# RWKV and mLSTM in one trunk kernel: the layout of the inverse blocks, the rows of the low rate weights, and the place of a normalisation

## The chip, the cores and the metric

The kernel runs on one core of one Trainium2 chip. The metric is the device time of one execution, from its start to its end, in microseconds (us). An execution that was recorded with the hardware profiler also has a span, from its first to its last instruction.

## The reference, cut to what matters

The program computes one decoder layer for a prompt (16 meta tokens and 1024 rows) and for eight sample sequences of eight rows, with model width 1024. One input projection feeds two mixers. Their gated sum goes through an output projection, a layer norm, a convolutional feed-forward block and a second layer norm. Everything is float32. Three pieces of it bear on this change.

```python
def _head_norm(h, eps):                      # mLSTM: over the 256 values of a head and row
    mu = jnp.mean(hf, -1, keepdims=True)
    var = jnp.mean(jnp.square(hf - mu), -1, keepdims=True)
    return (hf - mu) * lax.rsqrt(var + eps)
...
h = num / jnp.maximum(jnp.abs(den), jnp.exp(-m_row))[..., None]      # mLSTM, then _head_norm
...
w_log = -jax.nn.softplus(-(w0 + jnp.tanh(xw) @ w2)) - 0.5            # RWKV rates: rank 64
a = jax.nn.sigmoid(a0 + xa @ a2)                                     # rank 64
...
S = S * w[:, :, None, :] + sa[..., None] * (kk * a)[:, :, None, :] + v[..., None] * k[:, :, None, :]
```

The RWKV recurrence on the last line runs over all rows for 16 heads of 64. The kernel does it in chunks of 64 rows, and for that it needs the inverse of a unit triangular 64x64 matrix for each head and chunk.

## The kernel before, in words

**Passes.** The 1090 rows that count (sample, meta, prompt) are worked in three passes of up to 384 columns. Weights are split into a high part of type fp32r and a low remainder, and a dense product is three matmuls (high by high, high by low, low by high), called by `mm3`, which ends in line 57. So nearly all matmuls have line 57 in the profile, and are told apart by their tiles.

**Stage one, 0 to about 420 us: mLSTM.** For each pass and each of four heads `mlstm_qkv` makes q, k and v (dense products into the PSUM tile `d`), and `mlstm_head` works three tiles of 128 rows. For a tile it forms the weighted scores `wt`, the sum of the inner and the carried part into `hraw` (line 552, VectorE), and the new state `C1` (line 577, VectorE, read by the next tile's matmul). When the three tiles are done, the head is normalised: mean and variance of each tile (lines 585, 586), the denominators of all three tiles at once in four small VectorE operations (590 to 593), one power of -1/2 on GpSimd (594), and a subtract and multiply for each tile (596). Then TensorE transposes the tiles (606, 612), ScalarE scales them, and they go to HBM. In this stage the framework's list scheduler orders the instructions of every engine by its own model of their times; the order of the program is the priority. In all, 12 heads and 36 tiles are worked.

**Stage two, about 420 to 1610 us: RWKV with the gates.** Two of the 8 blocks of 128 channels make one unit `u`, so there are 4 units in each of 3 passes, 12 in all. The order on TensorE is written out by hand here (`rwkv`): a loop over units, each of 18 rounds, in which one step of the recurrence (`rwkv_chain`), pieces of the preparation of later units (`rwkv_g`, `rwkv_t`, `rwkv_mid`) and a share of the dense products (`dense`) are issued one after the other. The other engines are ordered by the list scheduler.

- `rwkv_k` loads the rank-64 weights of a block into `raw`, which holds them twice, in rows 0 to 63 and again in rows 64 to 127. ScalarE rounds all 128 rows of 256 columns into the high part (line 690), and GpSimd makes the low part in two instructions of 64 rows by 128 columns (693).
- `rwkv_r` forms the two rate products of a block (decay and in-context rate). The input `xwa[n]` holds the high part of the inputs in one half of the rows and the low part in the other. Each product is a matmul over 128 rows with the high weights, and one over 64 rows with the low weights (the loop of lines 715 to 719). There are 24 blocks, so 48 matmuls of each of the two forms.
- `rwkv_t` inverts the 32x32 diagonal blocks on VectorE (`LX`, lines 838 to 850). `rwkv_mid` transposes them (890, 892), forms the off-diagonal blocks on TensorE into the PSUM tile `gg`, and collects the inverse in `TT`. For that ScalarE copies with lines 918, 919 and 921. The tile is laid out as (2, 32, 12): a column of one 64x64 inverse is 12 elements, 48 bytes, from the next.
- `rwkv_chain` runs 6 steps for a unit. A step multiplies the right-hand side `Rs` by the inverse: four matmuls of 64x64 with `TT` as the stationary operand, in the loop over `up`. The profile has two records for a float32 matmul, so that is 8 records, 72 times. The matmuls of `VU` by `Gk` have the same form, 64x64 with 64 moving columns, and their stationary operand lies contiguous in SBUF.

**Stage three, to the end:** output projection, layer norms and the feed-forward block. The change does not touch it.

Of the kernel before, what the change touches and what calls it, by code (L numbers as in the profile page):

```python
# [8 lines left out]
F32 = mybir.dt.float32  # L9
F32R = mybir.dt.float32r  # L10
AF = mybir.ActivationFunctionType
ALU = mybir.AluOpType
# [31 lines left out]
class Trunk:  # L44
# [468 lines left out]
    def mlstm_head(self, pas, h, pool):  # L513
# [14 lines left out]
        for t in range(NT):  # L528
            c0, n = self.tcols(pas, t)
            cs = slice(c0, c0 + n)  # L530
            first = pas == 0 and t == 0
            ps = self.gh()
            fb = self.psc.tile([P, 512], F32, name="u")
            self.mm(ps[0:n, 0:n], k[:, cs], q[:, cs])
            self.mm(fb[0:n, 0:n], sel[:, h, 0:n], self.frow[:, cs])
            wt = pool.tile([P, 128], F32, name="wt", bufs=3)
            mask = self.const("tri0", slice(0, 90)) if first else self.const("tri")
            nc.vector.scalar_tensor_tensor(wt[0:n, 0:n], fb[0:n, 0:n], CT[0:n, t, 0, h:h + 1], mask,
                                           op0=ALU.add, op1=ALU.add)
            nc.scalar.activation(wt[0:n, 0:n], wt[0:n, 0:n], AF.Exp)  # L540
            nc.vector.tensor_tensor(wt[0:n, 0:n], ps[0:n, 0:n], wt[0:n, 0:n], op=ALU.mult)
            pn = self.psc.tile([P, 512], F32, name="y", bufs=2)
            self.mm(pn[0:n, 0:257], wt[0:n, 0:n], V1[0:n, t, 0:257])
            pi = self.psc.tile([P, 512], F32, name="y", bufs=2)
            if first:
                for b in range(8):
                    self.mm(pi[0:n, 0:257], self.qm[:, b * 90:(b + 1) * 90], C0[:, b, 0:257], b == 0, b == 7)
            else:
                self.mm(pi[0:n, 0:257], q[:, cs], C1[:, h, 0:257])
            it = pool.tile([P, 258], F32, name="it", bufs=3)  # L550
            nc.scalar.activation(it[0:n, 0:257], pi[0:n, 0:257], AF.Copy, scale=CT[0:n, t, 1, h:h + 1])
            nc.vector.tensor_tensor(hraw[0:n, t, 0:257], pn[0:n, 0:257], it[0:n, 0:257], op=ALU.add)

            pk = self.gh()
            nc.tensor.transpose(pk[0:n, 0:128], k[:, cs], ident)
            if first:
                wm = pool.tile([P, 9], F32, name="wm")
                nc.vector.tensor_scalar(wm[0:n, :], self.const("rm9", slice(0, n)), CT[0:n, t, 3, h:h + 1], None, op0=ALU.mult)
                km = pool.tile([P, 9, 128], F32, name="km")
                nc.vector.tensor_tensor(km[0:n], pk[0:n, 0:128].unsqueeze(1).broadcast_to([n, 9, 128]),  # L560
                                        wm[0:n].unsqueeze(2).broadcast_to([n, 9, 128]), op=ALU.mult)
                for b in range(9):
                    pc = self.psc.tile([P, 512], F32, name="u") if b % 2 else self.pst.tile([P, 512], F32, name="t")
                    self.mm(pc[:, 0:257], km[0:n, b, :], V1[0:n, t, 0:257])
                    if b < 8:
                        nc.vector.scalar_tensor_tensor(C0[:, b, 0:257], C0[:, b, 0:257], dec[:, h, NM + b:NM + b + 1],
                                                       pc[:, 0:257], op0=ALU.mult, op1=ALU.add)
                    else:
                        nc.scalar.copy(C1[:, h, 0:257], pc[:, 0:257])
                nc.sync.dma_start(out=self.o["C_s"][h], in_=C0[:, :, 0:257])  # L570
            else:
                tm = t - 1 if pas == 0 else t
                kw = pool.tile([P, 128], F32, name="kw", bufs=2)
                nc.scalar.activation(kw, pk[:, 0:128], AF.Copy, scale=CT[:, t, 3, h:h + 1])
                pc = self.pst.tile([P, 512], F32, name="t")
                self.mm(pc[:, 0:257], kw, V1[:, t, 0:257])
                nc.vector.scalar_tensor_tensor(C1[:, h, 0:257], C1[:, h, 0:257], dec[:, h, tm:tm + 1],
                                               pc[:, 0:257], op0=ALU.mult, op1=ALU.add)
        if pas == NPASS - 1:
            nc.sync.dma_start(out=self.o["C_p"][h], in_=C1[:, h, 0:257])  # L580

        mv = pool.tile([P, 3, 2], F32, name="mv", bufs=2)
        for t in range(NT):
            st = pool.tile([P, 6], F32, name="bst", bufs=2)
            nc.vector.bn_stats(st, hraw[:, t, 0:256])
            nc.vector.bn_aggr(mv[:, t, :], st)
        dn = pool.tile([P, 3], F32, name="dn", bufs=2)
        den = hraw[:, 0:NT, 256]
        stt = nc.vector.scalar_tensor_tensor
        stt(dn[:, 0:NT], den, -1.0, den, op0=ALU.mult, op1=ALU.max)  # L590
        nc.vector.tensor_tensor(dn[:, 0:NT], dn[:, 0:NT], CT[:, 0:NT, 2, h], op=ALU.max)
        stt(dn[:, 0:NT], dn[:, 0:NT], LN_EPS, dn[:, 0:NT], op0=ALU.mult, op1=ALU.mult)
        nc.vector.tensor_tensor(dn[:, 0:NT], dn[:, 0:NT], mv[:, 0:NT, 1], op=ALU.add)
        nc.gpsimd.tensor_tensor(dn[:, 0:NT], dn[:, 0:NT], self.const("mhalf")[:, 0:NT], op=ALU.pow)
        for t in range(NT):
            nc.vector.tensor_scalar(hraw[:, t, 0:256], hraw[:, t, 0:256], mv[:, t, 0:1], dn[:, t:t + 1],
                                    op0=ALU.subtract, op1=ALU.mult)
        off = W * pas
        for cb in range(2):
            j = 2 * h + cb  # L600
# [55 lines left out]
    def rwkv_static(self, pool):  # L656
        nc = self.nc
        r = {}
        r["TT"] = [pool.tile([P, 2, 32, 12], F32, name=f"TT{n}") for n in range(2)]
        for t in r["TT"]:  # L660
            nc.gpsimd.memset(t, 0.0)
        r["Gd"] = pool.tile([P, 404], F32, name="Gd")
        nc.gpsimd.memset(r["Gd"], 0.0)
        r["LX"] = pool.tile([P, 32, 32], F32, name="LX")
        r["n2"] = pool.tile([P, 32], F32, name="n2")
        nc.vector.memset(r["n2"], 0.0)
        self.ones = pool.tile([P, 128], F32R, name="ones")
        nc.scalar.copy(self.ones, self.const("bones"))
        self.r = r
# [6 lines left out]
    def rwkv_k(self, pas, j, w, pool):  # L676

        nc, i = self.nc, self.i
        m = j % 2
        st = self.st[pas, j] = {}  # L680
        RA = pool.tile([P, NP, 4, 64], F32, name="RA", bufs=6)
        KB = pool.tile([P, NP, 4, 64], F32, name="KB", bufs=6)

        one, two = slice(0, 4, 3), slice(1, 3)
        rs, bs = (two, one) if m else (one, two)
        st.update(RA=RA, KB=KB, r=RA[:, :, rs, :], k=KB[:, :, rs, :], a=RA[:, :, bs, :], b=KB[:, :, bs, :])
        raw = self.wpool.tile([P, 512], F32, name="raw", bufs=3)[:, 0:256]
        nc.sync.dma_start(out=raw, in_=i["lora2"][j, :, 0:256])
        lw = [self.rs.tile([P, n], F32R, name=f"lw{n}", bufs=2) for n in (256, 128)]
        nc.scalar.copy(lw[0], raw)  # L690
        for q in (0, 64):
            a, c = slice(q, q + 64), slice(2 * q, 2 * q + 128)
            nc.gpsimd.tensor_tensor(lw[1][a], raw[a, c], lw[0][a, c].bitcast(F32), op=ALU.subtract)
        yield from self.lerp(pas, w, 8 + j, self.pt[:, j, 1:2], self.pd[:, j, 1:2], st["k"], pool)
        st["lw"] = lw

    def rwkv_r(self, pas, j, w, pool):
# [15 lines left out]

        zs = self.gbank()
        for n in range(2):
            rows = slice(64 * n, 64 * n + 64)
            x, ps = self.xwa[n], zs[:, n, 0:W]
            self.mm(ps, lw[0][:, 2 * rows.start:2 * rows.start + 128], x, True, False)
            self.mm(ps, lw[1][rows], x[rows], False, True)
        for n, (dst, bias) in enumerate(((cw, dv(3)), (ta, dv(4)))):  # L720
            act(dst, zs[:, n, 0:W], AF.Tanh, bias=bias, scale=0.5)
        for _ in range(4):
# [157 lines left out]
    def rwkv_mid(self, pas, u, pool):  # L880
# [34 lines left out]

        yield from (m0 + 0.11 for _ in product(A21, Tn, 0, 32, lambda w, h1: nc.scalar.copy(P1[h1], w[h1])))
        for q in (0, 64):
            nc.scalar.copy(TT[q:q + 32, 0, :, cs], Tx[q:q + 32, :, cs])
        nc.scalar.copy(TT[:, 1, :, cs], Tx[:, :, cs])
        yield m0 + 0.165  # L920
        yield from (m0 + 0.22 for _ in product(P1, Tx, 32, 0, lambda w, h0: nc.scalar.copy(
            TT[h0, 1, :, cs].rearrange("p t c -> p c t"), w[h0])))
        if pas == 0:

            yield m0 + 0.23
# [17 lines left out]
    def rwkv_chain(self, pas, u, pool):  # L943
# [30 lines left out]
        for p in range(NP):  # L974
            nxt = []
            for e in range(2):
# [30 lines left out]
                up, sp = yr[:, 256:384], yr[:, 384:512]  # L1007
                for h in range(2):
                    for m in range(2):
                        self.mm(up[brs[m], hh[h]], TT[brs[m], :, :, 6 * m + h * NP + p], Rs[brs[m], hh[h]], meta, True, True)  # L1010
                for m in range(2):
                    nc.scalar.copy(now[m][0][brs[m], e, :], up[brs[m], :])
                if p + 1 < NP:
# [715 lines left out]
```

## Time and profile before

| | |
|---|---|
| three timed runs | 2534.26 us median (2525.82 to 2535.51) |
| the profiled execution, its time | 2531.55 us |
| the profiled execution, its span | 2529.8 us, 43736 instructions |
| TensorE matmuls busy | 2361.2 us (93%), mean granted clock 0.968 of full speed |
| TensorE weight loads busy | 2125.8 us (84%), beside the matmuls |
| VectorE busy | 1549.8 us (61%) |
| ScalarE busy | 1078.4 us (43%) |
| GpSimd busy | 481.2 us (19%) |
| DMA | 356.97 MB, mean 141 GB/s |

In the rows of the profile PE is a TensorE matmul, PEld a weight load, DVE VectorE, ACT ScalarE and POOL GpSimd. A row of a timeline gives the start in us from the beginning of the span, the length in us, engine, line, operation, the tile written, the tiles read, the part of the TensorE array that is used, the shape and the number of records merged into the row. What stands in brackets is how long the engine sat idle before it, and what ended that. "issue" is idle time for which the profile shows no wait.

### The profile page before, as it was taken

The numbers are of one execution on the slowest core, as the hardware profiler recorded it, in microseconds if no ns is written. First come the engines' busy times: TensorE is split into PE (matmuls) and PEld (weight loads), VectorE is DVE, ScalarE is ACT, GpSimd is POOL, SyncE is SP. The second block draws the span as 40 slices with busy tenths as digits, with TensorE's granted clock in tenths as the row PEclk, the third lists the DMA queues.
The fourth block names the chain that finished last, engine by engine and source line by source line (L and its number), as shares of the span: only waits on it lengthen the run. The fifth ranks groups of instructions, "written<-read, shape, count | busy, mean of one in ns | idle before, by whom it ended". The sixth has DMA issues, their size and how long they took to land.

```text
span 2529.8 us, 43736 instructions
## 1 busy us (share of the span) xinstructions
PE 2361.2 (93%) x16303; PEld 2125.8 (84%) x16303; DVE 1549.8 (61%) x3367; ACT 1078.4 (43%) x2454; POOL 481.2 (19%) x669
## 2 busy tenths in 40 slices
PE   6999998879889989999989999888999999999997
PEld 6788897868777878887878888788999999999996
DVE  6555545997986787775887763456434433333437
ACT  4343444435545546656545555445313223132222
POOL 5000014644552201111111113121000000000003
PEclk9899998989999989999999999999999999999999
DMA  8463533645457455566445566884111111111112
GB/s 279 135 199 100 183 126 120 193 141 173 149 170 235 137 164 185 176 198 224 140 146 182 178 210 210 264 297 155 59 30 55 44 37 55 32 57 38 47 38 82
DMA packets 212508, 356.97 MB, mean 141 GB/s; under 512 B 24626, under 2 KB 83890, under 8 KB 212295
## 3 DMA queue, kind: packets, MB, share of 16 engines
q1 hardware_dynamic: 212295, 354.17, 44.0%
q8 instruction: 128, 2.10, 0.4%
q14 instruction: 85, 0.70, 0.1%
HBM read 272.00 MB, written 82.08 MB: 140 GB/s over the span
## 4 chain that ended last, share of the span: by engine, by line
PE 48%; DVE 5%; DMA 4%; ACT 1%; issue 1%; SPq 0%; POOL 0%; DVEq 0%; ACTq 0%
PE d L57 33%; PE y L57 12%; PE gg L57 2%; DMA mg_d<-mA 1%; DVE acc L128 1%; PE t L57 1%; DMA tho<-mA_d 1%; DMA raw<-mg_d 0%; DVE S L1046 0%; DVE Gd L812 0%; DMA mA<-gA_d 0%; DVE tm L845 0%; DVE acc L1552 0%; PE t L960 0%; DVE LX L847 0%
## 5 line engine op out<-in xcount | busy, mean ns | idle before, releaser
L57 PE MATMUL d<-Xh,whi 128*128 128x384 f32 (+3 forms) x1544 | 554.4, 359 | 12.6 <-ACT sm L1144 6.3
L57 PE MATMUL d<-Xl,whi 128*128 128x384 f32 (+3 forms) x1544 | 526.6, 341 | 2.2 <-DMA Xl<-xl_d 1.9
L57 PE MATMUL d<-Xh,wlo 128*128 128x384 f32 (+3 forms) x1544 | 524.7, 340 | 1.5 <-DMA wlo<-lo_w_out_b 0.9
L57 PE MATMUL d<-X1h,whi 128*128 128x364 f32 (+2 forms) x1120 | 371.1, 332 | 3.7 <-ACT whi L90 2.4
L57 PE MATMUL d<-X1h,wlo 128*128 128x364 f32 (+3 forms) x1120 | 370.8, 331 | 0.0
L57 PE MATMUL d<-X1l,whi 128*128 128x364 f32 (+3 forms) x1120 | 370.0, 331 | 0.0
L57 PEld LDWEIGHTS d<-Xh,whi 128*128 128x128 f32 (+1 forms) x1544 | 299.2, 194 | 37.2 <-ACT sm L1144 7.1
L57 PEld LDWEIGHTS d<-Xl,whi 128*128 128x128 f32 (+1 forms) x1544 | 299.8, 194 | 5.9 <-DMA Xl<-xl_d 4.3
L57 PEld LDWEIGHTS d<-Xh,wlo 128*128 128x128 f32 (+1 forms) x1544 | 299.0, 194 | 3.9 <-DMA wlo<-lo_w_out_b 1.5
L73 ACT CAST whi<-raw 128x512 fp32r<-128x512 f32 (+1 forms) x255 | 156.9, 617 | 311.6 <-PE d L57 256.8
L57 PEld LDWEIGHTS d<-X1h,whi 128*128 128x128 f32 x1120 | 212.0, 189 | 9.0 <-ACT whi L90 3.1
L57 PEld LDWEIGHTS d<-X1l,whi 128*128 128x128 f32 x1120 | 211.8, 189 | 5.1 <-DVE X1l L1374 0.2
L57 PEld LDWEIGHTS d<-X1h,wlo 128*128 128x128 f32 x1120 | 212.2, 189 | 3.3
L1552 DVE TENSOR_TENSOR acc<-y,acc 128x512 f32<-128x512 f32 (+1 forms) x144 | 97.7, 687 | 167.7 <-PE y L57 167.7
L74 DVE TENSOR_TENSOR wlo<-raw,whi 128x512 fp32r<-128x512 f32 (+1 forms) x135 | 98.7, 734 | 155.4 <-ACT whi L73 154.9
L74 POOL TENSOR_TENSOR wlo<-raw,whi 128x512 fp32r<-128x512 f32 x120 | 163.2, 1362 | 154.2 <-ACT whi L73 96.9
L90 ACT CAST whi<-raw 128x512 fp32r<-128x512 f32 x232 | 143.0, 618 | 111.1 <-PE d L57 63.1
L847 DVE TENSOR_TENSOR LX<-LX,tm 128x30 f32<-128x30 f32 (+4 forms) x360 | 146.3, 406 | 9.6
L57 PE MATMUL y<-wdh,hh 128*128 128x512 f32 x352 | 138.8, 394 | 5.4 <-DVE acc L1552 5.4
L845 DVE TENSOR_TENSOR tm<-LX 128x30 f32<-128x30 f32 (+4 forms) x360 | 135.2, 376 | 9.3
L57 PE MATMUL y<-wdl,hh 128*128 128x512 f32 x352 | 138.4, 393 | 0.0
L57 PE MATMUL y<-wdh,hl 128*128 128x512 f32 x352 | 138.3, 393 | 0.0
(364 smaller groups left out, 4176.6 us busy)
## 6 DMA issues: line engine op xcount, KB each, us to landing
raw<-in_w_up_dram SPq DMA_DIRECT2D x88, 256.0 KB, 2.8
raw<-in_wv_dram SPq DMA_DIRECT2D x48, 256.0 KB, 3.2
raw<-in_wk_b_dram SPq DMA_DIRECT2D x48, 256.0 KB, 3.8
raw<-in_wr_dram SPq DMA_DIRECT2D x48, 256.0 KB, 3.4
raw<-in_wv_b_dram SPq DMA_DIRECT2D x48, 256.0 KB, 3.0
raw<-in_wgb_dram SPq DMA_DIRECT2D x48, 256.0 KB, 3.4
raw<-in_wo_dram SPq DMA_DIRECT2D x48, 256.0 KB, 3.5
raw<-in_wga_dram SPq DMA_DIRECT2D x48, 256.0 KB, 3.5
```

Of the source, the lines that this page charges most:

```text
L57: self.nc.tensor.matmul(out, lhsT, rhs, start=start, stop=stop, skip_group_check=skip)
L73: nc.scalar.copy(hi[:, :n], src[:, u:u + n])
L74: self.lo_eng.tensor_tensor(lo[:, :n], src[:, u:u + n], hi[:, :n].bitcast(F32), op=ALU.subtract)
L90: nc.scalar.copy(hi, raw)
L128: nc.vector.scalar_tensor_tensor(y, y, rs[r], g[u][r], op0=ALU.mult, op1=ALU.mult)
L845: tt(tv_, LX[:, s + 1:, s:s + 1].broadcast_to([P, m, s]), LX[:, s:s + 1, 0:s].broadcast_to([P, m, s]), op=ALU.mult)
L847: tt(LX[:, s + 1:, 0:s], LX[:, s + 1:, 0:s], tv_, op=ALU.add)
L1552: tt(acc[0:m, t, ns], ps[0:m], acc[0:m, t, ns], op=ALU.add)
```

## The change

Three edits.

1. `TT` is declared as (12, 2, 32) and not (2, 32, 12), so that one 64x64 inverse lies in 64 consecutive elements of each row. The ScalarE copies of lines 918 and 919 now read with a step of 32 elements and write contiguously. The copy of line 921 was contiguous in its reading and had a step of 12 in its writing; it is now contiguous on both sides.
2. The low part of the rate weights is formed on all 128 rows, by one GpSimd instruction of 128x256 for two of 64x128, and kept in one buffer (two before). The high part keeps two. Both matmuls of a rate product are now 128 rows by 128 columns.
3. In the mLSTM head the normalisation of a tile stands right behind the tile's sum, ahead of the state update, with the denominators, the power and the scaling done for each tile by itself.

```diff
@@ mlstm_head, behind line 552
+            st = pool.tile([P, 6], F32, name="bst", bufs=2)
+            mv = pool.tile([P, 2], F32, name="mv", bufs=3)
+            nc.vector.bn_stats(st, hraw[:, t, 0:256])
+            nc.vector.bn_aggr(mv, st)
+            dn = pool.tile([P, 1], F32, name="dn", bufs=3)
+            den = hraw[:, t, 256:257]
+            stt = nc.vector.scalar_tensor_tensor
+            stt(dn, den, -1.0, den, op0=ALU.mult, op1=ALU.max)
+            nc.vector.tensor_tensor(dn, dn, CT[:, t, 2, h:h + 1], op=ALU.max)
+            stt(dn, dn, LN_EPS, dn, op0=ALU.mult, op1=ALU.mult)
+            nc.vector.tensor_tensor(dn, dn, mv[:, 1:2], op=ALU.add)
+            nc.gpsimd.tensor_tensor(dn, dn, self.const("mhalf")[:, 0:1], op=ALU.pow)
+            nc.vector.tensor_scalar(hraw[:, t, 0:256], hraw[:, t, 0:256], mv[:, 0:1], dn, op0=ALU.subtract, op1=ALU.mult)
...
-        (lines 582 to 597: the same for the three tiles of a head together)
@@ rwkv_static
-        r["TT"] = [pool.tile([P, 2, 32, 12], F32, name=f"TT{n}") for n in range(2)]
+        r["TT"] = [pool.tile([P, 12, 2, 32], F32, name=f"TT{n}") for n in range(2)]
@@ rwkv_k
-        lw = [self.rs.tile([P, n], F32R, name=f"lw{n}", bufs=2) for n in (256, 128)]
-        nc.scalar.copy(lw[0], raw)
-        for q in (0, 64):
-            a, c = slice(q, q + 64), slice(2 * q, 2 * q + 128)
-            nc.gpsimd.tensor_tensor(lw[1][a], raw[a, c], lw[0][a, c].bitcast(F32), op=ALU.subtract)
+        lw = [self.rs.tile([P, 256], F32R, name=f"lw{n}", bufs=b) for n, b in (("h", 2), ("l", 1))]
+        self.parts(raw, *lw, nc.gpsimd)
@@ rwkv_r
-            rows = slice(64 * n, 64 * n + 64)
             x, ps = self.xwa[n], zs[:, n, 0:W]
-            self.mm(ps, lw[0][:, 2 * rows.start:2 * rows.start + 128], x, True, False)
-            self.mm(ps, lw[1][rows], x[rows], False, True)
+            for l in lw:
+                self.mm(ps, l[:, 128 * n:128 * n + 128], x, l is lw[0], l is lw[1])
@@ rwkv_mid
         for q in (0, 64):
-            nc.scalar.copy(TT[q:q + 32, 0, :, cs], Tx[q:q + 32, :, cs])
-        nc.scalar.copy(TT[:, 1, :, cs], Tx[:, :, cs])
+            nc.scalar.copy(TT[q:q + 32, :, 0, :], Tx[q:q + 32, :, cs].rearrange("p t c -> p c t"))
+        nc.scalar.copy(TT[:, :, 1, :], Tx[:, :, cs].rearrange("p t c -> p c t"))
         yield m0 + 0.165
         yield from (m0 + 0.22 for _ in product(P1, Tx, 32, 0, lambda w, h0: nc.scalar.copy(
-            TT[h0, 1, :, cs].rearrange("p t c -> p c t"), w[h0])))
+            TT[h0, :, 1, :], w[h0])))
@@ rwkv_chain
-                        self.mm(up[brs[m], hh[h]], TT[brs[m], :, :, 6 * m + h * NP + p], Rs[brs[m], hh[h]], meta, True, True)
+                        self.mm(up[brs[m], hh[h]], TT[brs[m], 6 * m + h * NP + p], Rs[brs[m], hh[h]], meta, True, True)
```

`parts(src, hi, lo, eng)` copies `src` to `hi` on ScalarE and puts `src - hi` into `lo` on the engine named.

## Rows read from the trace of the kernel before

**Rows 1.** the stretches' busy time: us; PE, PEld, DVE, ACT, POOL (count); PEclk; DMA
```profile
0.00:420.00 420.00, 377.15 (x2273) 333.02 (x2273) 230.20 (x592) 176.17 (x396) 68.76 (x99) 0.96 0.52 163
420.00:560.00 140.00, 118.06 (x803) 107.38 (x803) 126.58 (x280) 60.10 (x132) 77.98 (x109) 0.89 0.54 168
...
850.00:1200.00 350.00, 335.20 (x2836) 294.49 (x2836) 264.93 (x638) 196.17 (x483) 50.25 (x94) 0.98 0.59 188
1200.00:1500.00 300.00, 278.84 (x2393) 244.66 (x2393) 242.81 (x588) 164.98 (x411) 46.11 (x66) 0.97 0.52 165
```

**Rows 2.** waits of the weight loads from 420 to 1610 us: total, times, longest
```profile
PEld gg L57 <- DVE T L892: 28.9, 3, 13.9
...
PEld y L57 <- ACT Yt L1048: 19.1, 27, 3.2
```

**Rows 3.** timeline of the weight loads, from 588.2 and from 591.3 us: start, us
```profile
588.30 0.31 PEld L57 LDWEIGHTS y<-VU,Gk 64*64 64x64 f32 x8 [0.17 <-issue]
588.69 0.19 PEld L57 LDWEIGHTS t<-cst,sq 128*128 128x128 f32 x1
...
591.48 0.62 PEld L57 LDWEIGHTS y<-Rs,TT 64*64 64x64 f32 x8 [0.21 <-issue]
592.17 0.14 PEld L960 LDWEIGHTS t<-cst,v 128*128 128x128 f32 x1
```

**Rows 4.** weight loads by form, 420 to 1610 us: busy, mean ns
```profile
L57 PEld LDWEIGHTS y<-Rs,TT 64*64 64x64 f32 x576 | 44.4, 227 | 18.5 <-issue 14.5 <-ACT Rs L1005 1.5 <-ACT sm L325 0.5
...
L57 PEld LDWEIGHTS y<-VU,Gk 64*64 64x64 f32 x576 | 22.6, 134 | 13.2 <-issue 12.3 <-ACT Yt L1048 0.9
```

**Rows 5.** timeline of the weight loads around one rate product
```profile
817.06 0.19 PEld L57 LDWEIGHTS gg<-xw,lw 128*128 128x128 f32 x1
817.50 0.18 PEld L57 LDWEIGHTS gg<-xw,lw 64*128 64x128 f32 x1 [0.25 <-issue]
...
818.61 0.19 PEld L57 LDWEIGHTS d<-Xh,whi 128*128 128x128 f32 x1 [0.19 <-issue]
```

**Rows 6.** timeline of the weight loads around one output-gate product
```profile
1030.02 0.19 PEld L57 LDWEIGHTS t<-xgh,lwgl 128*128 128x128 f32 x1
1030.19 0.19 PEld L57 LDWEIGHTS d<-Xh,whi 128*128 128x128 f32 x1
```

**Rows 7.** instructions on TT: duration ns min/median/max, first and last start
```profile
L918 ACT COPY TT<-T x24: 494/508/512, 525.6 to 1492.5; 32x384 f32<-32x384 f32 x24
L921 ACT COPY TT<-gg x24: 813/854/880, 544.9 to 1544.5; 32x384 f32<-32x384 f32 x24
L919 ACT COPY TT<-T x12: 511/513/517, 526.7 to 1493.0; 128x384 f32<-128x384 f32 x12
```

**Rows 8.** instructions on the PSUM tile gg, the copy of line 916
```profile
L916 ACT COPY A<-gg x24: 469/472/474, 535.3 to 1535.2; 32x384 f32<-32x384 f32 x24
```

**Rows 9.** instructions on lw; costliest groups, line 74 on POOL
```profile
L693 POOL TENSOR_TENSOR lw<-raw,lw x48: 445/462/1204, 371.8 to 1392.6; 64x128 fp32r<-64x128 f32 x48
...
L74 POOL TENSOR_TENSOR wlo<-raw,whi 128x512 fp32r<-128x512 f32 x120 | 163.2, 1362 | 154.2 <-ACT whi L73 96.9
```

**Rows 10.** instructions on dn and on hraw
```profile
L596 DVE TENSOR_SCALAR hraw<-hraw,mv,dn x36: 395/410/416, 104.2 to 415.5; 128x256 f32<-128x256 f32 x36
...
L593 DVE TENSOR_TENSOR dn<-dn,mv x12: 161/161/165, 103.1 to 413.7; 128x3 f32<-128x3 f32 x12
L594 POOL TENSOR_TENSOR dn<-dn,cst x12: 848/850/883, 103.3 to 414.0; 128x3 f32<-128x3 f32 x12
...
L585 DVE BATCH_NORM_STATS2 bst<-hraw x36: 407/428/430, 80.5 to 412.8; 128x6 f32<-128x256 f32 x36
```

**Rows 11.** timeline of DVE, last head of the last pass
```profile
412.35 0.43 DVE L552 TENSOR_TENSOR hraw<-y,it 128x257 f32<-128x257 f32 x1
...
414.87 1.06 DVE L596 TENSOR_SCALAR hraw<-hraw,mv,dn 128x256 f32<-128x256 f32 x3 [0.97 <-POOL dn L594]
```

**Rows 12.** waits of PE matmuls up to 420 us: total, times, longest
```profile
PE g L612 <- DVE hraw L596: 7.4, 3, 3.7
```

More of the change, by code (lines that the diff above doesn't have):

```diff
@@ L580, in mlstm_head @@
             nc.sync.dma_start(out=self.o["C_p"][h], in_=C1[:, h, 0:257])
[L582 to L597, printed above, removed]
         off = W * pas
```

## Prediction, made before the changed kernel was run

> **What bounds the kernel now.** I read the busy times by stretch first, then the waits, then the timeline of the weight loads, because the question is which engine's work sets the pace where each edit lands. [Rows 1] give four stretches; the reader should compare TensorE's busy time with the length. From 850 to 1200 us TensorE is busy 335.2 of 350 us, at a granted clock of 0.98, so nearly all of it at the upper level, 2.4 GHz. VectorE is second, with 264.9. From 1200 to 1500 us it is 278.8 against 242.8 of 300. So stage two runs at TensorE's pace, with VectorE not far behind, except at its start: from 420 to 560 us VectorE is busy 126.6 of 140 us. [Rows 2] show where TensorE's weight loads stand still there: 28.9 us in 3 long waits for VectorE's transposed inverse (one at the start of each pass), and 27 short ones for the copy of the chain's output, 19.1 us. What is cut from TensorE's instruction stream in stage two should therefore nearly all come off the end, as long as VectorE and those three waits leave room. In stage one TensorE is also the busiest, 377.2 of 420 us, against 230.2 for VectorE and 68.8 for GpSimd [rows 1].
>
> **Edit 1, the inverse blocks.** [Rows 3] show two groups of the same form, 8 records of 64x64 with 64 moving columns. The group on Gk starts at 588.30 and the next weight load at 588.69: 0.39 us. The group on TT starts at 591.48 and the next load at 592.17: 0.69 us. Nothing in either waits for another engine. One weight load takes 227 ns on TT and 134 ns on Gk, over 576 of each [rows 4]. The one difference that I see is the step of 48 bytes between the columns of TT. With TT contiguous I take Gk's duration: 0.69 - 0.39 = 0.30 us a group, 72 groups (576 / 8), 21.6 us off TensorE. Bounds: 0 (the step is not the cause) and 21.6.
>
> The Trainium skill, "TensorE: Matmul & The Clock Gate", section "LDWEIGHTS (loading the stationary operand)", gives the time of a weight load by its number of columns alone. By that rule the two groups would cost the same and this edit would bring nothing; the trace does not agree, with 227 against 134 ns for 64 columns each, and I go by the trace.
>
> The price is on ScalarE, which writes TT. Line 921 has taken 854 ns with a stepped write [rows 7] and should take the 472 ns of line 916, the same number of elements copied contiguously from PSUM [rows 8]: 24 x 0.38 = 9.2 us less. Lines 918 and 919 (508 and 513 ns, 36 in all [rows 7]) now read with a step. No row shows a stepped read on ScalarE; I bound it by no change and by the stepped write, 854 ns, which costs 36 x 0.34 = 12.3 us. Both together are between 9.2 us less and 3.1 us more, on an engine that is busy 196 of 350 us [rows 1], and TT is made long before its step. I take zero on the path; the cover is TensorE's dense work, and without it at most 3.1 us would show.
>
> **Edit 2, the rate weights.** [Rows 5] show one block's four matmuls: first load at 817.06, the load behind the group at 818.61, so 1.55 us. The form changes between 128 and 64 rows at each step, and each step shows idle time without a wait (0.25 us, then 0.19). [Rows 6] show the same width, 384 moving columns with 128x128 weights, with no change of form: 0.17 us from 1030.02 to 1030.19. Four such steps are 0.68 us. I take 1.55 - 0.68 = 0.87 us, 24 blocks, 20.9 us off TensorE. Bounds: 0 (the idle time is not from the change of form) and 20.9. GpSimd has one instruction of 256 columns for two of 128 columns. A line through 462 ns at 128 columns and 1362 ns at 512 [rows 9] gives an estimate of 0.76 us for 0.92, between 0.46 and 1.36: 24 times at most 0.44 us, 10.6 us, on an engine busy 50 of 350 us [rows 1]. The single buffer makes this instruction wait for the last block's rate product. That stands at the start of the block's last dense product, a whole product earlier, so I price the wait at zero; if it came, the low parts of the dense weights would queue behind it on GpSimd, and TensorE would wait for those.
>
> **Edit 3, the mLSTM normalisation.** The work on the 256 columns stays: 36 statistics, 36 scalings [rows 10]. The four small VectorE operations (161 ns for the longest) and the power (850 ns) were done 12 times and are now done 36 times [rows 10]: 24 x 4 x 0.16 = 15.4 us more on VectorE, 24 x 0.85 = 20.4 us more on GpSimd, in a stretch where they are busy 230 and 69 of 420 us [rows 1]. Each scaling stands behind a power, as the 0.97 us of idle time in [rows 11] shows: up to 24 more such waits, 23 us, in VectorE's queue, with the score weights, the state update and the low parts of the dense weights behind them. In front of TensorE lie the next head's dense products, so I take zero there. What can be gained is at the end of the last pass, where no dense work is left: TensorE waited 7.4 us in 3 places for the scaled tiles [rows 12]. The chain from a sum to its first scaling is the same; the other two scalings, 1.06 - 0.41 = 0.65 us [rows 10, 11], leave the path for the last two heads. I take 1.3 us. Bounds: 7.4 us gained, 10 us lost (some 0.3 us for each tile).
>
> **The sum.** TensorE's stream gets 21.6 + 20.9 = 42.5 us shorter in stage two. Not all comes through. The three waits for the inverse end when VectorE ends; what is cut in the time of VectorE's chain before them makes them longer instead (about a unit's length, two or three TT groups and one or two blocks: about 1.5 us each, 4 us in all). VectorE's share from 850 to 1200 us goes from 76% to 79% when 12 us leave that stretch, and I give 4 us for short waits that grow. That leaves 34.5 us, and with edit 3 it is 35.8 us. The profiled execution took 2531.55 us (its span 2529.8), so 2531.6 - 35.8 = 2495.8; the median of the runs shown is 2.7 us above that execution, and I say 2497.
>
> **Rivals.**
> - *VectorE takes over in stage two.* For it: it is busy 126.6 of 140 us at the start [rows 1]. Against it: from 1200 to 1500 us it still has a fifth of the time free (242.8 of 300) [rows 1]. If half of the 42.5 us turns into longer waits, 2531.6 - 21 = 2510.
> - *The step is not the cause* (the page's rule): edit 2 alone, at the forecast's share of 34.5 / 42.5 = 0.81, is 17 us, so 2514. The 93 ns between two loads of one size [rows 4] speak against it.
> - *Edit 2 doesn't do what it says*, and the idle time stays: edit 1 alone, 17.5 us, so 2513. The 0.17 us of [rows 6] speak against it.
> - *Slower: VectorE's queue holds up the mLSTM chain.* The power's wait stands ahead of the state update, which the next tile's matmul needs. The price is at most 2.5 us a tile (from the end of the sum at 412.78 to the end of a scaling, 414.87 + 0.41 [rows 11]), 36 tiles, 90 us: 2531.6 - 34.5 + 90 = 2587. It decides from (34.5 + 12.7) / 36 = 1.3 us of TensorE idle time a tile on. For it: TensorE has no other work at the end of the last pass. Against it: VectorE is free for 190 us of the stage, and the list scheduler can put other work ahead of the wait.
>
> **How the numbers follow.** About 0.5%, 12.7 us, is what a measurement of this kernel can tell from no change. Forecast (28 to 45 us gained) 0.64; VectorE takes over 0.14; step not the cause 0.05; edit 2 without effect 0.05; slower 0.05; more than 45 us, because waits shrink with the stream, 0.07. Faster by over 12.7 us: 0.64 + 0.07 and most of the next three, 0.17, is 0.88; same: the rest of those three, 0.07; slower 0.05. The range goes from full passage with some of edit 3's gain, 2531.6 - 42.5 - 5 = 2484, to the two cases in which one edit does nothing with a few us lost in edit 3, 2518.
>
> **What would show it.** In the changed kernel the loads on TT should take about 134 ns and a TT group 0.39 us; a block's rate products four loads of 128 rows 0.17 us apart, without idle time inside; line 921 near 0.47 us; 36 powers in place of 12, and TensorE's idle time up to 420 us not longer. The waits for the transposed inverse should be a few us longer than 28.9. It is wrong if TT's loads stay above 200 ns, if the idle time at the rate products stays, or if stage one ends later than before.

## The result, and the profile after

The changed kernel takes 2517.44 us (median of 4 runs, 2512.73 to 2519.16), the kernel before 2534.89 us beside it: a ratio of 0.9935, with a 95% interval of 0.9912 to 0.9959. By that ratio it is 16.5 us faster (the medians differ by 17.5) where 35.8 were forecast. The profiled execution took 2519.16 us (span 2517.0, mean granted clock 0.963 where it was 0.968).

TensorE's instructions became shorter just as forecast. The weight loads by form, from 414 to 1600 us, answer to [rows 4], and the two timelines of the weight loads answer to [rows 3, 5]:

```profile
L57 PEld LDWEIGHTS y<-Rs,TT 64*64 64x64 f32 x576 | 23.2, 138 | 19.3 <-issue 13.5 <-ACT Rs L998 1.5 <-ACT whi L90 1.0
```

```profile
558.07 0.31 PEld L57 LDWEIGHTS y<-Rs,TT 64*64 64x64 f32 x8 [0.21 <-issue]
558.45 0.14 PEld L953 LDWEIGHTS t<-cst,v 128*128 128x128 f32 x1
...
1048.97 0.19 PEld L57 LDWEIGHTS gg<-xw,lwh 128*128 128x128 f32 x1
1049.15 0.19 PEld L57 LDWEIGHTS gg<-xw,lwl 128*128 128x128 f32 x1
...
1049.69 0.19 PEld L57 LDWEIGHTS d<-Xh,whi 128*128 128x128 f32 x1
```

A TT group takes 0.38 us (0.69 before), and a block's four rate products take 1049.69 - 1048.97 = 0.72 us (1.55 before), with no idle time inside. Over 72 groups and 24 blocks that is 22 and 20 us, 42 us of TensorE time.

Stage two did not become 42 us shorter. I take it from the first rate product to the last TT group. The busy times of that stretch (columns as in [rows 1]), in the kernel before and in the changed one:

```profile
417.80:1595.00 1177.20, 1090.97 (x9144) 956.07 (x9146) 899.61 (x2085) 622.65 (x1551) 341.04 (x472) 0.96 0.57 179
```

```profile
414.70:1585.00 1170.30, 1068.14 (x9145) 949.49 (x9146) 904.21 (x2085) 625.81 (x1551) 339.14 (x451) 0.95 0.57 181
```

The stretch is 1177.2 us before and 1170.3 us after, 7 us shorter. Length less matmul time gives the time without a matmul: 86.2 us before, 102.2 us after, so 16 us of the 42 came back as idle time. The granted clock of the trace stands at its lower level, 1.2 GHz, for 88.9 us of the stretch before and for 124.7 us after. That is half the upper level, so I estimate the cost of the 35.8 us more at half of them, some 18 us. The matmul time bears this out: it fell by 1090.97 - 1068.14 = 22.8 us where the instructions became 42 us shorter, and the difference is 19. 42 - 16 - 18 = 8 us, against 7 measured. The other 5.8 us of this execution's shorter span (2529.8 to 2517.0) lie outside: 3.1 in stage one, the rest behind the last TT group.

Where TensorE stands still now, by the waits of its weight loads in the stretch (total us, times, longest); the first two rows answer to [rows 2]:

```profile
PEld gg L57 <- DVE T L885: 29.1, 3, 14.1
PEld y L57 <- ACT Yt L1041: 24.5, 27, 3.4
...
PEld t L57 <- ACT sq L728: 7.3, 5, 3.0
```

The long waits for the inverse, where I had put 4 us, did not grow (28.9 before). The short ones did: the copy of the chain's output (`Yt`) from 19.1 [rows 2], and the squares of the keys (`sq`, a tile that ScalarE writes and a matmul reads at the end of a block) from 1.7 (the same view of before):

```profile
PEld t L57 <- ACT sq L735: 1.7, 2, 0.9
```

One such place shows how a wait for the squares comes about. In the timeline of ScalarE the copies into TT take 2.78 us in a row, and the squares come at the end of a run of work without a pause. TensorE arrives before them (timeline of the weight loads):

```profile
1048.50 1.85 ACT L911 COPY TT<-T 32x384 f32<-32x384 f32 x2 [0.71 <-DVE T L883]
1050.36 0.93 ACT L912 COPY TT<-T 128x384 f32<-128x384 f32 x1
...
1055.26 0.78 ACT L728 ACTIVATE sq<-KB,pt 128x192 f32<-128x192 f32 x2
```

```profile
1056.10 0.74 PEld L57 LDWEIGHTS t<-cst,sq 128*128 128x128 f32 x6 [1.36 <-ACT sq L728]
```

Right behind it the granted clock falls; this is the stretch from 1058 to 1062 us, whose clock column says 0.57:

```profile
1058.00:1062.00 4.00, 4.00 (x25) 3.55 (x26) 2.68 (x9) 2.29 (x5) 0.21 (x1) 0.57 0.25 93
```

In the kernel before, the copies at the same place took 1.03 + 0.51 = 1.54 us, and the row of TensorE's loads of the squares shows no wait (timelines of ScalarE and of the weight loads):

```profile
1054.75 1.03 ACT L918 COPY TT<-T 32x384 f32<-32x384 f32 x2 [0.72 <-DVE T L890]
```

```profile
1062.30 0.81 PEld L57 LDWEIGHTS t<-cst,sq 128*128 128x128 f32 x6
```

ScalarE's copies as instructions on TT, edit 3 as those on dn (answering to [rows 7, 10]), and the wait of [rows 12] among TensorE's waits, each from the changed kernel:

```profile
L911 ACT COPY TT<-T x24: 842/899/947, 524.7 to 1482.3; 32x384 f32<-32x384 f32 x24
L914 ACT COPY TT<-gg x24: 468/471/475, 543.8 to 1533.3; 32x384 f32<-32x384 f32 x24
L912 ACT COPY TT<-T x12: 850/877/927, 526.5 to 1483.2; 128x384 f32<-128x384 f32 x12
```

```profile
L565 POOL TENSOR_TENSOR dn<-dn,cst x36: 550/551/917, 81.1 to 412.1; 128x1 f32<-128x1 f32 x36
```

```profile
PE g L609 <- DVE hraw L566: 7.1, 4, 2.2
```

### The profile page after: what moved, and what is told of

The parts are those of the page before. It is cut to its first block, busy times and chain, and to the rows that moved or that the text cites. A ratio compares the mean times of both kernels' runs of the same rounds, so it can differ in the third digit from the quotient of the medians.

```text
span 2517.0 us, 43818 instructions
## 1 busy us (share of the span) xinstructions
PE 2333.4 (93%) x16303; PEld 2115.5 (84%) x16303; DVE 1568.3 (62%) x3463; ACT 1080.9 (43%) x2454; POOL 488.4 (19%) x669
## 4 chain that ended last, share of the span: by engine, by line
PE 43%; DVE 8%; DMA 3%; ACT 3%; issue 2%; SPq 0%; POOL 0%; DVEq 0%; ACTq 0%; POOLq 0%
PE d L57 30%; PE y L57 11%; PE gg L57 1%; DVE tm L838 1%; DVE LX L840 1%; DVE S L1039 1%; DMA tho<-mA_d 1%; DVE acc L128 1%; PE t L57 1%; DMA o_d<-sm 0%; DMA mg_d<-mA 0%; ACT whi L90 0%; DVE Gd L805 0%; DMA xr<-xs_d 0%; DVE acc L1545 0%
## 5 line engine op out<-in xcount | busy, mean ns | idle before, releaser
L838 DVE TENSOR_TENSOR tm<-LX 128x30 f32<-128x30 f32 (+4 forms) x360 | 141.3, 393 | 9.4
```

The costliest lines, as they stand in the source:

```text
L838: tt(tv_, LX[:, s + 1:, s:s + 1].broadcast_to([P, m, s]), LX[:, s:s + 1, 0:s].broadcast_to([P, m, s]), op=ALU.mult)
```

## The experiments

All ratios are to the kernel before on the same chip, with 95% intervals. The runs of one kernel spread over some 10 to 25 us, so an interval is about 0.4% wide, 10 us (the difference of two such ratios has one of some 8 us either way), and differences of a few us between two variants are not settled by it.

**Each edit alone.** `e1_tt` is the kernel before with edit 1, `e2_lora` with edit 2, `e3_norm` with edit 3, `e12` with edits 1 and 2. Their lines are those of the diff above, for instance in `e1_tt`:

```diff
-        r["TT"] = [pool.tile([P, 2, 32, 12], F32, name=f"TT{n}") for n in range(2)]
+        r["TT"] = [pool.tile([P, 12, 2, 32], F32, name=f"TT{n}") for n in range(2)]
...
```

> Edit 1 alone (TT contiguous, the rest as before). In the changed kernel the 72 TT groups are 0.31 us shorter each, 22 us of TensorE time, and still only about 9 us of stage two's 38 us came through between the first and the last TT group. Theory W (what TensorE is freed of turns into waits for ScalarE and VectorE, and into stretches at the lower clock that such waits bring): edit 1 alone gains 6 to 14 us, with idle time and lower-clock time in stage two both above before's. Theory S (the stepped ScalarE copies of lines 918 and 919, now about 0.9 us each where they took 0.5, hold up the chain): edit 1 alone gains under 4 us, and edit 2 alone keeps nearly all of its 20. Theory P (each edit passes in full and edit 3 takes it back): 18 to 22 us.

> Edit 2 alone (rate weights on 128 rows). 24 groups are 0.85 us shorter, 20 us of TensorE time. Theory W: gains 6 to 12 us, and the wait of the matmul on sq (line 735) grows from 1.7 us, since the group stands at the start of the block whose end waits for sq. Theory S: gains 15 to 20 us, because no ScalarE work is added. Theory P: 18 to 20 us.

> Edit 3 alone (mLSTM normalised behind each sum). The changed kernel reaches the first rate product 3.1 us earlier than before (414.7 against 417.8 us), of which at most 1 us can be from the other edits, which do nothing in stage one. Theories W and S: between 2 and 4 us faster, inside the noise of the measurement. Theory P: slower by some 20 us.

> Edits 1 and 2 without edit 3. Theories W and S: gains 9 to 16 us, 3 us less than all three edits, and under W clearly less than the sum of the two edits alone. Theory P: gains 35 to 40 us.

Measured: `e1_tt` 0.9945 (0.9922 to 0.9967), 14 us; `e2_lora` 0.9975 (0.9955 to 0.9996), 6 us; `e3_norm` 0.9975 (0.9961 to 0.9989), 6 us; `e12` 0.9946 (0.9927 to 0.9964), 14 us. Edit 1 keeps about two thirds of its 22 us, edit 2 a third of its 20, and on top of edit 1 nothing that can be measured. Edit 3 takes nothing back. S and P fall. Theory W (waits and the lower clock) is the one that fits; that `e12` is less than the sum of the two edits (14 against 20 us) is within the noise, and edit 3 gained more than any of them said.

The traces show which edit brought the waits. With edit 2 alone, the waits for the copy of the chain's output and for the squares are already as long as with all three edits, or nearly so (from 415 to 1595 us in `e2_lora`):

```profile
PEld y L57 <- ACT Yt L1044: 25.0, 30, 2.9
...
PEld t L57 <- ACT sq L731: 5.5, 3, 4.1
```

With edit 1 alone, stepped copies and all, they are 18.8 and 2.3 us, as before. The stretch without a matmul says the same: 3 us more with edit 1 alone, 10 us more with edit 2 alone. So it is mainly edit 2 that TensorE pays for with waits. A TT group is a step of the chain whose output it waits for, so edit 1 also brings that output forward, and edit 2 only brings TensorE to it sooner; this reason is argued and was not tested.

**ScalarE's copies relieved.** `a_pool` has the stepped copies on GpSimd. `a_cont` stores the transposed inverse block by block, so that they read contiguously:

```diff
@@ a_pool
-            nc.scalar.copy(TT[q:q + 32, :, 0, :], Tx[q:q + 32, :, cs].rearrange("p t c -> p c t"))
-        nc.scalar.copy(TT[:, :, 1, :], Tx[:, :, cs].rearrange("p t c -> p c t"))
+            nc.gpsimd.tensor_scalar(TT[q:q + 32, :, 0, :], Tx[q:q + 32, :, cs].rearrange("p t c -> p c t"), 1.0, None, op0=ALU.mult)
+        nc.gpsimd.tensor_scalar(TT[:, :, 1, :], Tx[:, :, cs].rearrange("p t c -> p c t"), 1.0, None, op0=ALU.mult)
@@ a_cont
-        nc.vector.transpose(Tx, LX)
+        nc.vector.transpose(Tx.rearrange("p c t -> p t c"), LX)
...
-            nc.scalar.copy(TT[q:q + 32, :, 0, :], Tx[q:q + 32, :, cs].rearrange("p t c -> p c t"))
-        nc.scalar.copy(TT[:, :, 1, :], Tx[:, :, cs].rearrange("p t c -> p c t"))
+            nc.scalar.copy(TT[q:q + 32, :, 0, :], Tx[q:q + 32, cs, :])
+        nc.scalar.copy(TT[:, :, 1, :], Tx[:, cs, :])
...
```

> The changed kernel with the three stepped copies of a unit (lines 911 and 912, 32.1 us of ScalarE in all) on GpSimd. Theory A (ScalarE's queue: the copies stand ahead of the squares, tanh and copies that TensorE comes to sooner now): the wait on sq falls from 7.3 us to under 3, idle time between the first and the last TT group falls from 76.9 us towards before's 64, and the whole gains 6 us or more on the changed kernel (ratio to before 0.991 or less). Theory V (VectorE takes over): no change or slower, ratio 0.993 to 0.997, since GpSimd and VectorE get nothing back. Theory C (only the clock's drops differ): ratio 0.993 with the same idle time.

> The changed kernel with the transposed inverse stored block by block, so that lines 911 and 912 read contiguously (about 0.5 us each again, 14 us less on ScalarE), and the transpose of line 883 writes with a step (by the row of line 885, 1.985 against 1.241 us, 12 times, 9 us more on VectorE). Theory A: 3 to 8 us faster than the changed kernel, ratio to before 0.990 to 0.992. Theory V: slower than the changed kernel by a few us, ratio 0.994 to 0.998. Theory C: as the changed kernel, 0.993.

Measured: `a_pool` 0.9947 (0.9924 to 0.9969), with the wait for sq at 9.5 us: against A. `a_cont` 0.9910 (0.9886 to 0.9935), where A put it. The interval also reaches C's 0.993 and stays just below V's range; that of `c_again` below, the same kernel once more, reaches into all three. The copies of line 911 took 512 ns in `a_cont`, as long as before the change. The wait for sq is 6.1 us there, the wait for the chain's copy 25.5: both much as in the changed kernel.

**VectorE unloaded.** `b_nolx` is the kernel before and `a_nolx` the changed kernel, both without the elimination steps of `rwkv_t`; `n1` and `n2` add edit 1 or edit 2 alone to `b_nolx`.

```diff
...
-            tt(tv_, LX[:, s + 1:, s:s + 1].broadcast_to([P, m, s]),
-               LX[:, s:s + 1, 0:s].broadcast_to([P, m, s]), op=ALU.mult)
-            tt(LX[:, s + 1:, 0:s], LX[:, s + 1:, 0:s], tv_, op=ALU.add)
```

> The changed kernel without the 720 elimination steps of rwkv_t on VectorE (lines 838 and 840, 283 us of VectorE), which leaves the inversion out. To be read against the same omission in the kernel before. Theory V: VectorE's load was what took the gain back, so without it the difference between the two kernels is 33 to 45 us. Theory A: the difference stays at 12 to 22 us, since ScalarE's queue is as it was.

> The kernel before without the same 720 elimination steps, which leaves the inversion out. Theories A and V: faster than before by the three long waits for the inverse, 25 to 60 us; the difference to the changed kernel with the same omission is 33 to 45 us under V and 12 to 22 us under A.

> Edit 1 alone on the kernel before without the elimination steps on VectorE (the inversion left out). With them, edit 1 was worth 14 us of its 22. Theory V (VectorE's load, and the waits and lower clock that come of it, took the gain): 18 to 24 us faster than the kernel before with the same omission (0.9799 of before), so 0.9705 to 0.973. Theory A (ScalarE's stepped copies take it): 10 to 15 us, 0.974 to 0.976.

> Edit 2 alone on the kernel before without the elimination steps on VectorE (the inversion left out). With them, edit 2 was worth 6 us of its 20, and nothing on top of edit 1. Theory V: 14 to 20 us faster than 0.9799 of before, so 0.972 to 0.9745. Theory A: up to 8 us, since the squares that TensorE waits for stand in ScalarE's queue all the same: 0.977 to 0.980.

Measured: `b_nolx` 0.9799 (0.9769 to 0.9829), `a_nolx` 0.9673 (0.9649 to 0.9697): 28 us between their medians (2477.24 and 2449.59), 32 by the ratios, give or take 10, where the kernels with the elimination differ by 16.5. That lies between what A (12 to 22) and V (33 to 45) said, and does not decide between them. `n1` came to 0.9771 (0.9747 to 0.9795) and `n2` to 0.9770 (0.9752 to 0.9788), 7 us each from `b_nolx`, on another chip and with some 10 us of noise either way: V's ranges lie below both intervals, A's reach into both. The stretch in the profiled executions of `b_nolx` and `a_nolx`:

```profile
420.70:1547.20 1126.50, 1083.09 (x9144) 948.22 (x9146) 645.87 (x1365) 625.04 (x1551) 336.52 (x472) 0.98 0.59 187
```

```profile
407.80:1505.40 1097.60, 1043.03 (x9144) 929.12 (x9146) 644.12 (x1365) 623.97 (x1551) 338.59 (x451) 0.98 0.60 192
```

Here stage two is 28.9 us shorter for 42 us of TensorE time. The idle time grew by 11 us (43.4 to 54.6), and the clock column is 0.98 in both. So with VectorE unloaded 11 us go into waits, where the forecast had 8 and its rival 21, and the lower clock takes little. These two executions are far apart in their sets, the first the second slowest of six and the second the fastest, and stage one differs by another 13 us in them (420.7 and 407.8), so 28.9 is an account of two executions and not of the kernels.

**One wait taken away.** `a_defer` issues the product on sq three dense steps later, `c_defer` does the same with `a_cont`'s reads. `c13` is `a_cont` without edit 2, and `a_again` the changed kernel beside them.

```diff
         n2 = r_["n2"]
-        ps = self.pst.tile([P, 512], F32, name="t")
...
+        def tail():
+            ps = self.pst.tile([P, 512], F32, name="t")
...
+        self.tail = [3, tail]
         yield
@@ dense
                     yield False
                     since += 1
+                    late(False)
```

> The changed kernel itself, beside the three below on one chip. All theories: ratio to before 0.992 to 0.995, with about 125 us at the lower clock and 103 us of TensorE idle time from the first rate product to the last TT group.

> The changed kernel with the product on sq (three matmuls a block) issued three dense steps later, so that TensorE has work while ScalarE squares. Theory A (the stepped copies and the shorter rate products make TensorE wait for ScalarE, and such waits bring stretches at the lower clock): the wait on sq falls from 7.3 us to under 2, the time at the lower clock in stage two falls by 7 us or more, and the whole gains 4 to 12 us on the changed kernel. Theory V (VectorE's load sets the length): the idle time moves to other waits, no gain (within 3 us).

> The later product on sq together with the contiguous reads of lines 911 and 912 (the transpose of line 883 writing with a step). Theory A: the gains add: 7 us and 4 to 12 us on the changed kernel, ratio to before 0.986 to 0.989. Theory V: as the contiguous reads alone, 0.991.

> Edits 1 and 3 with the contiguous reads of lines 911 and 912, without edit 2. With them edit 2 then stands alone between this kernel (no edit 2) and the one with contiguous reads and all three edits (0.991). Theory A: with ScalarE relieved, edit 2 is worth 6 to 12 us, so this one is at 0.9935 to 0.996. Theory V: edit 2 is worth nothing once TensorE is ahead of VectorE: 0.990 to 0.992.

Measured: `a_again` 0.9934 (0.9909 to 0.9958), `a_defer` 0.9946 (0.9925 to 0.9966), `c_defer` 0.9955 (0.9935 to 0.9975), `c13` 0.9921 (0.9902 to 0.9941). The wait for sq fell in `a_defer` from 8.0 us in 5 places (`a_again`) to 3.8 us in one, not to under 2, and others have grown by more:

```profile
PEld y L57 <- ACT Yt L1044: 31.8, 28, 3.4
...
PEld t L956 <- DVE n L761: 15.3, 5, 7.1
```

They are 25.6 and 10.3 us in `a_again`. A's gain did not come. But the second of these rows is VectorE's reading of the very product that was put off (line 761 takes it out of PSUM), so the edit moved part of the wait along its own chain, and `a_defer` does not tell what the squares alone are worth. `c13` lies at the upper end of V's range, with an interval that touches A's. Beside `a_cont` and `c_again`, on other chips, it makes edit 2 worth 3 and -2 us on top of the rest, give or take 8: little of its 20. Its waits are those of a kernel without edit 2, 19.2 us for the chain's copy and 2.1 for sq.

**Last attempts.** `c_again` is `a_cont` once more, `c_r` moves one VectorE product of the second and third pass to GpSimd, `a_split` and `c_split` put the copies of line 911 one and two rounds later.

```diff
@@ c_r
-        tt(r, r, Dv, op=ALU.mult)
+        (nc.gpsimd.tensor_tensor if pas else tt)(r, r, Dv, op=ALU.mult)
@@ a_split, behind the second product (they are gone from ahead of it)
+        for q in (0, 64):
+            nc.scalar.copy(TT[q:q + 32, :, 0, :], Tx[q:q + 32, :, cs].rearrange("p t c -> p c t"))
+            yield m0 + 0.24
```

> The changed kernel with contiguous reads in lines 911 and 912 and the stepped write in line 883 once more, as the best version so far (0.991 on the first chip). All theories: 0.989 to 0.993.

> The same as c_again with the product of r and the decay (line 749, 0.56 us on VectorE) on GpSimd in the second and third pass: 16 times, 9 us off VectorE, nothing left out. Theory V: 2 to 8 us faster than c_again. Theory A, or if the two engines get in each other's way: no gain or slower.

> The changed kernel with the three stepped copies of a unit no longer in a row: line 912 where it was, the two of line 911 one round and two rounds later. Theory A (bursts in ScalarE's queue, 2.78 us of copies ahead of what TensorE waits for): idle time in stage two falls by 5 us or more and the whole gains 3 to 8 us on the changed kernel, 0.990 to 0.992. Theory M (several queues are late in turn, so one relieved wait comes back as another): within 2 us of the changed kernel, 0.9925 to 0.995.

> The same with contiguous reads, as in c_again. Theory A: 0.989 to 0.991. Theory M: as c_again, 0.991 to 0.994.

Measured: `c_again` 0.9929 (0.9906 to 0.9952), `c_r` 0.9928 (0.9907 to 0.9948), `a_split` 0.9950 (0.9931 to 0.9968), `c_split` 0.9932 (0.9913 to 0.9951). None of them gains, clear of noise, on what it was made from. Theory M is what is left, that there is no single queue; it is left by exclusion, and `c_r`'s interval still takes in part of V's 2 to 8 us. The contiguous reads came to 0.9910 and 0.9929 in two sets, the changed kernel to 0.9935 and 0.9934. The version with contiguous reads beats the kernel before; that it beats the changed kernel is likely and not settled.

The accounts of stage two, one profiled execution each, first rate product to last TT group. Freed is the TensorE time by instructions; idle is length less matmul time; the clock's part is half the change of the time at the lower level. All are against the kernel before, or `b_nolx` where it is named. Sum and measured differ by up to 7 us, so a row tells nothing finer:

| kernel | freed | idle | clock's part | sum | measured |
|---|---|---|---|---|---|
| edit 1 (`e1_tt`) | 22 | +3 | +4 | -15 | -12 |
| edit 2 (`e2_lora`) | 20 | +10 | +3 | -7 | -4 |
| edits 1, 2 (`e12`) | 42 | +19 | +16 | -7 | -5 |
| changed kernel | 42 | +16 | +18 | -8 | -7 |
| changed kernel (`a_again`) | 42 | +19 | +6 | -17 | -15 |
| contiguous reads (`a_cont`) | 42 | +21 | +8 | -13 | -17 |
| the same without edit 2 (`c13`) | 22 | +8 | +5 | -9 | -16 |
| `a_nolx` against `b_nolx` | 42 | +11 | +3 | -28 | -29 |
| edit 1, `n1` against `b_nolx` | 22 | +4 | +2 | -16 | -17 |
| edit 2, `n2` against `b_nolx` | 20 | +9 | +6 | -5 | -5 |

Edit 2 brings 9 to 16 us of idle time in each pair of rows that differ by it (with and without edit 1, with contiguous reads, without the elimination), edit 1 alone 3 and 4, and 9 on top of edit 2.

## Why the prediction was right and wrong

**What bounds the kernel:** right as far as it went. Stage two runs at TensorE's pace, but with less room than the shares of [rows 1] let one think: 76% of VectorE and 56% of ScalarE are means, and the work that TensorE waits for can stand at the end of a run without a pause, like the 7.5 us of ScalarE in the place shown above (1048.50 to the end of the squares at 1056.04).

**Edits 1 and 2 on TensorE:** right in both terms. 0.31 us a TT group for 0.30, 0.83 us a block for 0.87. The step of 48 bytes and the change of form were the causes, so the two rivals that denied one of them fall. A load of the same 64 columns went from 227 to 138 ns. The rule of the Trainium skill ("TensorE: Matmul & The Clock Gate", "LDWEIGHTS (loading the stationary operand)") goes by columns alone, and the trace of the changed kernel does not agree with it either. The single buffer cost GpSimd 4.2 us in 2 waits, and no wait of TensorE for the low part shows, so that price of zero was right.

**Edit 1 on ScalarE:** the sum lay just outside its bounds (9.2 us less to 3.1 more). The stepped reads took 899 and 877 ns, a little over the upper bound of 854, so ScalarE got 24 x 0.39 + 12 x 0.36 - 24 x 0.38 = 4.6 us more work. "TT is made long before its step" leaves out what stands behind the copies in ScalarE's queue, such as the squares in the place shown. With contiguous reads the kernel came out 1 and 6 us faster in two sets, inside the noise; and with edit 1 alone the waits named above did not grow. So that these copies cost the path anything is not shown.

**Edit 3:** 1.3 us forecast, 6.3 measured alone (3 to 10), inside the bounds given. TensorE's wait for the scaled tiles is 7.1 us as before (7.4), so the step I named did not bring it. Stage one lasts 412.4 us on average over the 13 profiled executions with edit 3 and 417.1 over the 7 without. Single executions run from 408 to 421 us, with 17 to 45 us at the lower clock, so the difference of 4.7 us is not far above the noise. In these averages TensorE's idle time in the stage is 1.6 us less with edit 3 and the time at the lower clock 6.3 us less; half of that and the idle time make up the 4.7. What in the new order brings it was not tried. The power on one column took 551 ns for 850 on three, so GpSimd's extra work was 36 x 0.55 - 12 x 0.85 = 9.6 us for the 20.4 of the forecast. The slower rival (VectorE's queue holding up the chain) did not occur.

**The sum is where it failed**, in the step "VectorE's share goes from 76% to 79%, and I give 4 us for short waits that grow". The waits took 16 us in the profiled execution, where the sum had 8, 4 of them for the three long ones, and these did not grow at all. The short waits that did grow are for ScalarE (the chain's copy and the squares, 11 us together by the rows above), and they came with edit 2; the step judged them by VectorE's share. And the sum had no term for the clock, though the table of stretches shows it at 0.89 where TensorE waits most [rows 1]; it took another 18 us in that execution and 6 in a second one. Why it took 18 us once and 6 us once, at nearly the same idle time (102 and 106 us), stays open.

The result, 2517, lies just inside the range only because the range reached to the cases in which one edit does nothing, and because edit 3 brought some 5 us more than forecast, by another way than the step named for it: both are luck. Three small slips changed nothing: 2495.8 + 2.7 is 2498.5 and not 2497, 2531.6 - 17.5 is 2514 and not 2513, and 264.9 of 338 us is 78% and not 79%. In size the rivals "step not the cause", 2514, and "edit 2 without effect", 2513, are nearest, but both loads did become shorter. "VectorE takes over", 2510, is the next, and its cause is not shown: unloading VectorE brought the difference from 16.5 to some 30 us, give or take 10, and edit 2 brought the same idle time there (+9 us in `n2`, +10 in `e2_lora`). Unloading ScalarE brought at most a few us, and putting one wait off made others grow. That several queues are late in turn, each with little slack, fits all of it, and is left by exclusion. Why edit 2's time turns into waits and edit 1's mostly does not stays open, beyond the reason argued above.

The timed runs of `n1` and `n2` kept 7 us each, give or take 10, and `a_nolx` with all three edits about 30. With such noise and two chips that is no contradiction: the profiled executions kept 17 us of edit 1 and 5 of edit 2 in stage two.

## What to carry to other kernels

When an engine that is busy 93% of the time is made 2% faster, ask of every place where another engine's result meets it how late that result may come. Busy shares don't say; the last few us of that engine's queue before the meeting point do. Time cut out of the chain that TensorE waits for came through better here (edit 1) than time cut beside it (edit 2). And count a wait on TensorE as more than itself: in the accounts above the lower clock took another 0.2 to 1.2 us for each us by which the idle time grew.

## What the runs showed that I had not expected

- Idle time and the lower clock go together. In stage two the idle time and the time at the lower level were 43 and 46 us in `b_nolx`, 55 and 51 in `a_nolx`, 86 and 89 in the kernel before, 105 and 120 in `e12`. They are not one and the same: two executions of the changed kernel had 102 and 125, and 106 and 100. Which of the two brings the other was not tried.
- In these copies a read with a step of 128 bytes cost ScalarE about as much as a write with a step of 48: 899 against 854 ns for 384 elements. Without a step it is 512 ns from SBUF (`a_cont`) and 471 from PSUM (line 914).
- Moved to GpSimd, the same copies took longer (1556 ns, line 911 of `a_pool`) and brought no gain.
- VectorE's transpose of 128x1024 took 1.24 us contiguous and 1.99 us with a stepped write in `a_cont`. It added 9 us on VectorE, and the kernel was no slower for it (0.9910 and 0.9929).
